# Attention in a hybrid diffusion step: steps of two query tiles in a written-out rotation, the scores of two heads on the two halves of the array, and the left half of the output weights 512 columns wide

## The chip, the cores and the metric

The kernel runs on one core of one Trainium2 chip. The metric is device microseconds of one execution, median over the runs shown. The engines are TensorE (PE, with its weight loads as a row of their own, PEld), VectorE (DVE), ScalarE (ACT), GpSimd (POOL) and SyncE (SP), which issues most DMAs.

## The reference

Two layers of a backbone act on 128 context tokens and 1024 sample tokens of width 1024, in float32. Layer 0 projects the modulated input once (`h @ w_in`, 3584 columns) and feeds a convolution branch and an attention branch, both gated; their outputs side by side (512 + 512 columns) go through one 1024 x 1024 output projection. Layer 1 is a pooling mixer with its own 1024 x 1024 output projection. What the change touches is the attention of layer 0 and the two output projections:

```
q = rms_norm(q, q_norm); k = rms_norm(k, k_norm)          # 8 heads of 64
# context tokens (128): plain attention
p = softmax(q @ k.T * 64**-0.5);  y = p @ v
# sample tokens (1024, a 16 x 64 grid): each block of 16 columns of a row sees
# an 8-row x 32-column window of keys (256) and all 128 context keys, in one softmax
s_win = where(col_ok, q @ k_win.T * 64**-0.5 + bias, -inf)
s_ctx = q @ k_ctx.T * 64**-0.5
p = softmax(concat(s_win, s_ctx));  y = p_win @ v_win + p_ctx @ v_ctx
# each layer's end
z = concat(y_conv * silu(ga), y_att * silu(gb));  out = z @ w_out
y = x + gate * out
```

## The kernel before

Every large product in float32 is made of three products of rounded parts (`float32r`): a number is split into a high part `hi` and the rest `lo`, and `hi*hi + hi*lo + lo*hi` is summed in one PSUM bank. `split` (L183) makes the parts of a weight unit of 1024 columns per partition: a copy on ACT, a subtraction on DVE.

The program is a list of items (L1164 to L1205), each with the weights that it needs; `ensure` loads and splits weights one or two items ahead. Items before the attention project the input (L225, 384 moving columns a matmul, and L232, 256 columns). A scheduler of the language (`schedule_with_timeline_sim=True`) moves the instructions on every engine, so an engine's order isn't the order of the code. PSUM has eight banks: four under the name `mm`, two `tp`, two `cv`.

Attention works on pairs of heads, `pr` = 0 to 3, and for each pair on two halves of the grid, `hf` = 0 and 1, with four query tiles of 128 (`j` = 0 to 3) each: 32 calls of `attn_tile` (L873). In one call:

- L883: for each head `e` of the pair two matmuls of 512 keys. The first has 128 rows: the stationary operand holds the head's `q` high part in 64 partitions and its low part in the other 64, the moving operand holds the same `k` high part twice. The second has 64 rows, `q` high times `k` low.
- L889 on DVE adds the bias and takes the extreme of each row; L893 on ACT takes the exponential and its sum; L894 on DVE takes the reciprocal; L895 on POOL multiplies.
- L898 transposes the probabilities in four 128 x 128 matmuls a head into a `tp` bank, which ACT copies out (L899).
- L905 multiplies with the values, the two heads on the two column halves of the array, 128 columns a matmul; L913 on DVE multiplies the result into the gated `za`.

`prep` (L791) turns the normalised `q` and `k` of a pair round (L806, L819), splits them on POOL and DVE, and copies `k` high to the other 64 partitions by a DMA (L843). The keys of the context cache stand ahead of the 1024 keys and behind them. `attn_prompt` (L916) does the context tokens. `bias_load` (L744) and `v_load` (L778) fetch the next pair's bias and value windows through SP; the value windows have one pair of buffers.

The output projection of layer 0 is `out0` (L1022), of layer 1 `out1` (L1048), nine tiles of 128 tokens each. For each tile `out_right` (L1006) makes columns 512 to 1023 in 24 matmuls of 512 columns, `out_left` (L995) columns 0 to 511 in two blocks of 24 matmuls of 256 columns.

## Time and profile before

| | us |
|---|---|
| median of 3 runs | 1037.79 (1035.22 to 1043.5) |
| profiled execution: time, its span | 1037.07, 1035.3 |
| PE busy | 999.0 (96%) |
| DVE, ACT, POOL busy | 615.3 (59%), 421.7 (41%), 406.1 (39%) |
| first score matmul of the attention (L883) | 439.74 |
| first matmul of the output projection of layer 0 (L1010) | 579.96 |
| last value matmul of the attention (L905) | 602.4 |

The span is cut by PE's work: input projections to 439 us, attention from 439 to about 602, the output projection of layer 0 mixed in from 580 and alone from 607 to about 718, the matmuls of layer 1 to 929, its output projection to the end. The profiled execution lies 0.7 us under the median. PE's matmuls are pipelined: the time that one takes from its neighbours is read from start to start, not from its own duration, which is longer.

### The profile page before, as it was taken

The page shows a single profiled execution, that of the slowest core. Times are in us where ns is not written, and L with a number is a line of the kernel's source. Part 1 is how long each engine was busy: PE and PEld are TensorE (multiplying, and loading weights), DVE is VectorE, ACT ScalarE, POOL GpSimd, SP SyncE. Part 2 cuts the span into 40 slices and gives each one's busy share as a digit, 9 for nine tenths or more (in the row PEclk, how much of TensorE's full clock was granted, in tenths as well). Part 3 has the DMA queues.
Part 4 walks back from the last instruction along what each step waited for, and adds up shares of the span by engine and source line. Part 5 has one row for each costly group of instructions (what it writes and reads, how often), then busy time and mean ns, then how long its engine had stood idle before and what let it go on. Part 6 is the DMA issues. An engine that isn't in the chain of part 4 may idle for free.

```text
span 1035.3 us, 17567 instructions
## 1 busy us (share of the span) xinstructions
PE 999.0 (96%) x6732; PEld 897.6 (87%) x6732; DVE 615.3 (59%) x1315; ACT 421.7 (41%) x851; POOL 406.1 (39%) x529
## 2 busy tenths in 40 slices
PE   5897999999999999999998999999999999999998
PEld 3786888899999999956665689999999999998997
DVE  3577999999833444475675455466354455586322
ACT  3374666765211443276675633244222222231010
POOL 2264879998533110564673324452000000003322
PEclk9998999999999999999998999999999999999999
DMA  9969554144211101325338132133111111133221
GB/s 299 330 174 331 177 214 143 52 154 142 62 51 44 41 21 52 86 65 144 88 107 202 66 115 84 68 113 103 41 51 41 51 42 51 51 113 107 98 82 62
DMA packets 90223, 111.74 MB, mean 108 GB/s; under 512 B 10828, under 2 KB 77260, under 8 KB 90027
## 3 DMA queue, kind: packets, MB, share of 16 engines
q1 hardware_dynamic: 84587, 95.93, 29.8%
q0 software_dynamic: 3216, 12.32, 3.6%
q10 hardware_dynamic: 2336, 2.36, 0.7%
q8 instruction: 53, 0.87, 0.4%
q14 instruction: 31, 0.25, 0.1%
HBM read 94.64 MB, written 21.57 MB: 112 GB/s over the span
## 4 chain that ended last, share of the span: by engine, by line
PE 86%; DMA 8%; SPq 2%; DVE 2%; POOL 1%; issue 1%; ACT 0%; ACTq 0%; POOLq 0%; DVEq 0%
PE mm L225 36%; PE mm L232 15%; PE mm L1010 9%; PE mm L1000 9%; PE mm L883 4%; PE cv L905 4%; PE tp L898 3%; DMA wada<-in_w_ada 2%; PE mm L1155 2%; DMA tbias<-in_rpb 2%; PE tp L335 2%; DMA raw<-in_w_out 1%; DMA k<-k 1%; DMA vwin<-in_cache_v 1%; SPq L294 1%; DMA wad<-in_w_ada 1%
## 5 line engine op out<-in xcount | busy, mean ns | idle before, releaser
L225 PE MATMUL mm<-h,whi 128*128 128x384 f32 x1536 | 396.9, 338 | 1.2 <-ACT whi L186 1.0
L225 PEld LDWEIGHTS mm<-h,whi 128*128 128x128 f32 x1536 | 276.6, 188 | 8.2 <-ACT gr L467 2.6
L225 PE MATMUL mm<-h,wlo 128*128 128x384 f32 x768 | 257.3, 336 | 0.3 <-DVE wlo L187 0.3
L469 POOL TENSOR_TENSOR zc<-zc,gr 128x384 f32<-128x384 f32 x138 | 150.2, 1090 | 31.9 <-ACT gr L467 22.9
L232 PE MATMUL mm<-whi,h 128*128 128x256 f32 x864 | 157.1, 284 | 0.0
L225 PEld LDWEIGHTS mm<-h,wlo 128*128 128x128 f32 x768 | 144.3, 188 | 1.3 <-issue 0.7
L232 PEld LDWEIGHTS mm<-whi,h 128*128 128x128 f32 x864 | 135.1, 192 | 3.9 <-issue 2.0
L232 PE MATMUL mm<-wlo,h 128*128 128x256 f32 x432 | 122.2, 283 | 0.0
L1000 PE MATMUL mm<-whi,zs 128*128 128x256 f32 x576 | 108.6, 284 | 0.0
L187 DVE TENSOR_TENSOR wlo<-raw,whi 128x1024 fp32r<-128x1024 f32 (+1 forms) x56 | 69.1, 1236 | 52.7 <-ACT whi L186 52.5
L480 DVE SCALAR_TENSOR_TENSOR cv<-u,convw,cv 128x384 f32<-128x384 f32 (+2 forms) x208 | 95.1, 512 | 0.9
L1010 PE MATMUL mm<-wrh,zs 128*128 128x512 f32 x288 | 93.4, 394 | 0.5 <-POOL wrh L981 0.5
L1000 PEld LDWEIGHTS mm<-whi,zs 128*128 128x128 f32 x576 | 91.7, 191 | 1.3 <-issue 0.2
L1017 POOL TENSOR_TENSOR y<-y,og 128x512 f32<-128x512 f32 x34 | 49.5, 1459 | 101.1 <-DVE og L1015 95.3
L186 ACT CAST whi<-raw 128x1024 fp32r<-128x1024 f32 (+1 forms) x56 | 56.9, 1016 | 64.0 <-PE mm L225 23.6
L232 PEld LDWEIGHTS mm<-wlo,h 128*128 128x128 f32 x432 | 82.9, 192 | 0.0
L1000 PE MATMUL mm<-wlo,zs 128*128 128x256 f32 x288 | 81.4, 283 | 0.0
L467 ACT ACTIVATE gr<-u,convw 128x384 f32<-128x384 f32 (+2 forms) x128 | 64.3, 531 | 30.7 <-POOL zc L469 30.2
L895 POOL TENSOR_SCALAR p<-p,st 128x512 f32<-128x512 f32 x64 | 49.7, 783 | 48.9 <-DVE st L894 40.9
L1015 DVE TENSOR_TENSOR og<-mm,gr 128x512 f32<-128x512 f32 x34 | 23.2, 688 | 70.0 <-PE mm L1010 39.0
L1010 PEld LDWEIGHTS mm<-wrh,zs 128*128 128x128 f32 x288 | 53.8, 188 | 10.8 <-POOL wrh L981 0.7
L449 ACT ACTIVATE th<-mm 128x384 f32<-128x384 f32 x48 | 23.5, 489 | 84.6 <-PE mm L225 80.2
(197 smaller groups left out, 1539.5 us busy)
## 6 DMA issues: line engine op xcount, KB each, us to landing
raw<-in_w_in SPq DMA_DIRECT2D x28, 512.0 KB
wad<-in_w_ada SPq DMA_DIRECT2D x16, 768.0 KB
wada<-in_w_ada SPq DMA_DIRECT2D x16, 512.0 KB
raw<-in_w_in SPq DMA_DIRECT2D x32, 256.0 KB
raw<-in_w_out SPq DMA_DIRECT2D x16, 512.0 KB
vw<-vwin SPq DMA_DIRECT2D x8, 640.0 KB
y0scr<-y POOLq DMA_DIRECT2D x9, 512.0 KB, 3.0
y<-y0scr SPq DMA_DIRECT2D x9, 512.0 KB
```

The lines of the kernel that those rows point to most:

```text
L186: se.copy(hi[:, :n], raw[:, :n])
L187: ve.tensor_tensor(lo[:, :n], raw[:, :n], f(hi[:, :n]), ALU.subtract)
L225: te.matmul(out, wsl(units, a, k, c0, P), hsl(hs, b, k, g), start=(k == 0 and i == 0), stop=(k == nk - 1 and i == 2))
L232: te.matmul(out, hsl(hs, p, k, g, a, P), wsl(units, q, k, 0, 256), start=(k == 0 and i == 0), stop=(k == 7 and i == 2))
L467: se.activation(pr[:, o : o + n], src, AF.Copy, scale=w)
L469: gp.tensor_tensor(z, z, pr, ALU.add)
L480: ve.scalar_tensor_tensor(zp if k == 30 else acc, src, convw[:, c, k : k + 1], zp if k == NPTS[c] else acc, ALU.mult, ALU.add)
L883: te.matmul(bs[e].rearrange("p (r c) -> p r c", c=32), qs[e][h, qo], kv, start=(i == 0), stop=(i == 1))
L895: gp.tensor_scalar(p2[:, e, :], p2[:, e, :], st[:, 4 + e : 5 + e], 0.0, ALU.mult, ALU.add)
L1000: te.matmul(b[:, blk * 256 : (blk + 1) * 256], zs[p][:, k, :], wsl(WL[blk], q, k, 0, 256), start=(k == 0 and i == 0), stop=(k == 7 and i = ...
L1010: te.matmul(b, zs[p][:, k, :], WR[q][k // 3][:, k % 3, :], start=(k == 0 and i == 0), stop=(k == 7 and i == 2))
L1017: gp.tensor_tensor(yv, yv, t, ALU.add)
```

## The change

The attention is written as a rotation. Its unit is a step of two query tiles of one pair and half: 16 steps, `STEPS`. In turn `s` of the loop PE does the scores of step s+1, the values of step s-1 and the transposes of step s, and then a piece of work for the context tokens or for the next pair. On PE, ACT and DVE the instructions keep the order in which the code writes them (`manual_schedule`); POOL and SP are still ordered by the scheduler.

- Scores: `q` and `k` of both heads lie in one tile each, head 0 in partitions 0 to 63, head 1 in 64 to 127. A tile of queries takes three products a head of 64 rows each, 512 keys wide, and the two heads' matmuls stand next to each other and write different banks. The second copy of `k` high and its DMA are gone.
- `prep` is cut into five pieces, spread over the turns of the pair before. ACT writes the high part straight from PSUM, DVE the low part from PSUM; these wait in `cv` banks.
- Of a step's four blocks of transposed probabilities, three go to banks `tp`, `tp`, `cv` and are copied by ACT, the fourth goes to a `tp` bank again and is copied by DVE. Values of two tiles share one bank.
- The context tokens' attention is in four pieces, one a turn.
- Value windows have two pairs of buffers. The right half of the output weights of layer 0 is loaded ahead and split on POOL and DVE alone, a quarter in each turn of the last pair.
- `out_left` makes 512 columns in 24 matmuls; the weights of the left half come in units of two row blocks by 512 columns (last tile of layer 1: still 256).

```diff
-    def split(raw, n=WUNIT):
+    def split(raw, n=WUNIT, c=256):
...
-        return hi.rearrange("p (k c) -> p k c", c=256), lo.rearrange("p (k c) -> p k c", c=256)
+        return hi.rearrange("p (k c) -> p k c", c=c), lo.rearrange("p (k c) -> p k c", c=c)
...
+        if srcs and srcs[0].shape[1] == 512:
+            for k0 in range(0, srcs[0].shape[0] // P, 2):
+                raw = wp.tile([P, WUNIT], F32, tag="raw", bufs=2, name=nm("raw"))
+                sy.dma_start(raw.rearrange("p (k c) -> p k c", c=512), srcs[0][k0 * P : (k0 + 2) * P, :].rearrange("(k p) c -> p k c", p=P))
+                raws.append((raw, WUNIT, 512))
...
-    VS = (6, 7)
-    QS = ((2, 3), (10, 11), (2, 3), (10, 11))
-    KS = ((4, 5), (12, 14), (4, 5), (12, 14))
-    KL = 16
+    QS = ((2, 3), (10, 11))
+    KS = ((4, 5), (None, 12))
+    VS = ((6, 7), (14, 16))
...
+        def two_parts(b, hi, lo, sc_):
+            se.activation(hi, b, AF.Copy, scale=sc_)
+            return lambda: ve.scalar_tensor_tensor(lo, b, sc_, f(hi), ALU.mult, ALU.subtract)
+        def q_half(i):
+            if i == 0:
+                st["q"] = [slot(x, F32R, "q")[:, :D] for x in QS[pr % 2]]
+            b = bank("cv")
+            for t in range(4):
+                o = b.rearrange("p (j r c) -> p r j c", j=4, c=16)[:, 2 * t : 2 * t + 2, :, :]
+                te.transpose(out=o, in_=qk_at(4 * i + t, pr)[:, 0:P], identity=ident)
+            o = slice(i * 512, (i + 1) * 512)
+            return two_parts(b, st["q"][0][:, o], st["q"][1][:, o], qn8)
+        def k_half(i):
+            b = bank("cv")
+            for t in range(4):
+                te.transpose(out=b[:, t * P : (t + 1) * P], in_=qk_at(4 * i + t, pr)[:, P : 2 * P], identity=ident)
+            if i == 0:
+                st["k"] = [slot(x, F32R, "k") if x is not None else gr_tile(F32R)[:, :SLOT] for x in KS[pr % 2]]
             o = slice(256 + i * 512, 768 + i * 512)
+            return two_parts(b, st["k"][0][:, o], st["k"][1][:, o], kn)
+        def rest():
+            qc = tmp("qc")
+            ck = qc[:, 2 * P : 3 * P]
+            last["ck"] = sy.dma_start(ck, A["cache_k_0"][0].rearrange("m h d -> m (h d)")[:, pr * P : (pr + 1) * P]).ins
+            b = bank("cv")
+            te.transpose(out=b[:, 0:P], in_=qk_at(8, pr)[:, 0:P], identity=ident)
+            te.transpose(out=b[:, P : 2 * P], in_=qk_at(8, pr)[:, P : 2 * P], identity=ident)
+            te.transpose(out=b[:, 2 * P : 3 * P], in_=ck, identity=ident)
+            se.activation(qc[:, 0:P], b[:, 0:P], AF.Copy, scale=qn8)
+            se.activation(qc[:, P : 2 * P], b[:, P : 2 * P], AF.Copy, scale=kn)
+            cx = b[:, 2 * P : 3 * P].rearrange("p (r w) -> p r w", w=32).unsqueeze(2).broadcast_to([P, 4, 2, 32])
+            kh, kl = st["k"]
+            hv, lv = (x[:, 0:256].rearrange("p (r a w) -> p r a w", a=2, w=32) for x in (kh, kl))
+            se.copy(hv, cx)
+            qkT[pr] = (*st["q"], kh, kl, qc[:, : 2 * P])
+            def later():
+                ve.tensor_tensor(lv, cx, f(hv), ALU.subtract)
+                for x in (kh, kl):
+                    gp.tensor_scalar(x[:, 1280:1536], f(x[:, 0:256]), 1.0, 0.0, ALU.mult, ALU.add)
+            return later
+        return [lambda: q_half(0), lambda: q_half(1), lambda: k_half(0), lambda: k_half(1), rest]
...
+    def scores(step, mem=None):
...
+        def matmuls(i):
+            j = j0 + i
+            bs = [bank("mm"), bank("mm")]
+            qo = slice(hf * 512 + j * P, hf * 512 + (j + 1) * P)
+            for n, (q, k) in enumerate(((qh, kh), (qh, kl), (ql, kh))):
+                for e in range(2):
+                    kv = k[H[e], o : o + 1024].rearrange("p (r c) -> p r c", c=64)[:, :, CB[j] : CB[j] + 32]
+                    te.matmul(bs[e].rearrange("p (r c) -> p r c", c=32), q[H[e], qo], kv, start=(n == 0), stop=(n == 2))
+            if mem is not None:
+                ps.append(mem[:, i * 1024 : (i + 1) * 1024].rearrange("p (e k) -> p e k", e=2))
+            else:
+                ps.append(wp.tile([P, 2, 512], F32, tag="whi", bufs=4, name=nm("p")))
+            sts.append(small(8, "st"))
             for e in range(2):
+                ve.tensor_tensor_reduce(
+                    out=ps[i][:, e, :], in0=bs[e], in1=bias[hf, e][:, JT[j], :], scale=-1.0, scalar=3e38, op0=ALU.add, op1=ALU.min,
+                    accum_out=sts[i][:, e : e + 1],
+                )
+        def exp(i, e):
+            p, st = ps[i][:, e, :], sts[i]
+            se.activation(p, p, AF.Exp, bias=st[:, e : e + 1], scale=-1.0, accum_out=st[:, 2 + e : 3 + e])
+        def norm(i):
+            st = sts[i]
+            ve.reciprocal(st[:, 4:6], st[:, 2:4])
+            for e in range(2):
+                gp.tensor_scalar(ps[i][:, e, :], ps[i][:, e, :], st[:, 4 + e : 5 + e], 0.0, ALU.mult, ALU.add)
+        return matmuls, exp, norm, ps
...
+    def values(step, pts, vw):
+        pr, hf, j0 = step
         ob = bank("cv")
         order = (4, 0, 1, 2) if hf == 0 else (1, 2, 3, 4)
+        for i in range(2):
+            for n, x in enumerate(order):
+                for e in range(2):
+                    te.matmul(
+                        ob[64 * e : 64 * e + 64, i * P : (i + 1) * P], vw[j0 + i][x][:, 64 * e : 64 * e + 64],
+                        pts[i][:, e, n * P : (n + 1) * P], start=(n == 0), stop=(n == 3),
+                    )
+        def gate():
+            r = 0
+            for zp, m in za_tok(pr, hf * 512, 512):
+                nr = m // 64
+                zv = zp.rearrange("p (r c) -> p r c", c=64)[:, :, 16 * j0 : 16 * j0 + 32].rearrange("p r (j c) -> p r j c", j=2)
+                ov = ob[:, : 2 * P].rearrange("p (j r c) -> p r j c", j=2, c=16)[:, r : r + nr, :, :]
+                ve.tensor_tensor(zv, ov, zv, ALU.mult)
+                r += nr
+        return gate
...
+    def prompt_attention(pr):
+        qp = qkT[pr][4]
+        pp = tmp("pp")
+        st = small(8, "st")
+        def first():
+            bs = [bank("cv"), bank("tp")]
+            for e in range(2):
+                te.matmul(bs[e][:, :P], qp[64 * e : 64 * e + 64, :P], qp[64 * e : 64 * e + 64, P : 2 * P], start=True, stop=True)
+            for e in range(2):
+                ve.tensor_reduce(st[:, e : e + 1], bs[e][:, :P], AX.X, ALU.max)
+            ve.tensor_scalar(st[:, 2:4], st[:, 0:2], -1.0, None, ALU.mult)
+            for e in range(2):
+                se.activation(pp[:, e * P : (e + 1) * P], bs[e][:, :P], AF.Exp, bias=st[:, 2 + e : 3 + e], accum_out=st[:, 4 + e : 5 + e])
+        def second():
+            ve.reciprocal(st[:, 6:8], st[:, 4:6])
+            for e in range(2):
+                gp.tensor_scalar(pp[:, e * P : (e + 1) * P], pp[:, e * P : (e + 1) * P], st[:, 6 + e : 7 + e], 0.0, ALU.mult, ALU.add)
...
+        return first, second, third, fourth
+    STEPS = [(pr, hf, j0) for pr in range(4) for hf in range(2) for j0 in (0, 2)]
...
+        first = hold["S"] = scores(STEPS[0], gr_tile())
+        for i in range(2):
+            first[0](i)
+            for e in range(2):
+                first[1](i, e)
+            first[2](i)
+        E = mybir.EngineType
+        with tc.manual_schedule(engines={E.PE, E.Activation, E.DVE}):
...
+    def attention_steps():
+        n = len(STEPS)
+        sc_, vw, pts = {0: hold["S"]}, {0: hold["V"]}, {}
+        pieces, later, right = [], [], None
+        for s in range(n + 1):
+            i, pr = s % 4, s // 4
+            while later:
+                later.pop(0)()
+            nxt = None
+            if s + 1 < n:
+                nxt = sc_[s + 1] = scores(STEPS[s + 1])
+                nxt[0](0)
+                nxt[0](1)
+                nxt[1](0, 0)
+                nxt[1](0, 1)
+                nxt[1](1, 0)
+                if pr < 3 and i in (0, 2):
+                    bias_load(pr + 1, i // 2)
+            if i == 0 and pr < 4:
+                pieces = prep(pr + 1) if pr < 3 else []
+                prompt = prompt_attention(pr)
+            gate = values(STEPS[s - 1], pts.pop(s - 1), vw[STEPS[s - 1][0]]) if s else None
+            if nxt:
+                nxt[2](0)
+            if gate:
+                gate()
+            if s == n:
+                break
+            ps = sc_.pop(s)[3]
+            pt = pts[s] = [wp.tile([P, 2, 512], F32, tag="wlo", bufs=4, name=nm("pt")) for _ in range(2)]
+            tbs = [bank("tp"), bank("tp"), bank("cv")]
+            for x in range(3):
+                turn(tbs[x], ps[x // 2][:, x % 2, :])
+            for x in range(2):
+                se.copy(pt[0][:, x, :], tbs[x])
+            if nxt:
+                nxt[1](1, 1)
+            tb = bank("tp")
+            turn(tb, ps[1][:, 1, :])
+            se.copy(pt[1][:, 0, :], tbs[2])
+            ve.tensor_copy(pt[1][:, 1, :], tb)
+            if nxt:
+                nxt[2](1)
+            prompt[i]()
+            for piece in pieces[2 * i : 2 * i + 2]:
+                later.append(piece())
+            if i == 2 and pr < 3:
+                vw[pr + 1] = v_load(pr + 1)
+            if pr == 3:
+                if i == 0:
+                    right = load_right(0, (13, 15, 17, 2, 3, 4))
+                hold["R"] = next(right)
...
-                if k % 2:
+                if k % 2 and l:
                     se.copy(hi[k // 3][:, k % 3, :], rv[:, k - k0, :])
...
-    def out_left(zs, WL, blks=(0, 1)):
+    def out_left(zs, WL, c0=0, n=512):
         b = bank("mm")
-        for blk in blks:
-            for k in range(8):
-                for i, (p, q) in enumerate(((0, 0), (0, 1), (1, 0))):
-                    te.matmul(
-                        b[:, blk * 256 : (blk + 1) * 256], zs[p][:, k, :], wsl(WL[blk], q, k, 0, 256),
-                        start=(k == 0 and i == 0), stop=(k == 7 and i == 2),
-                    )
+        for k in range(8):
+            for i, (p, q) in enumerate(((0, 0), (0, 1), (1, 0))):
+                te.matmul(b[:, c0 : c0 + n], zs[p][:, k, :], WL[k // 2][q][:, k % 2, c0 : c0 + n], start=(k == 0 and i == 0), stop=(k == 7 and i == 2))
         return b
...
-    items.append(([A["w_out_0"][:, 0:256]], keep("L0")))
+    items.append(([A["w_out_0"][0:512, 0:512]], keep("L0")))
...
+    items.append(([A["w_out_0"][512:1024, 0:512]], keep("L1", go_out0)))
```

On PE the rows change so. A tile and a half in pair 1 before (L883 scores, L905 values, L898 transposes; `k_5261` and `k_5262` are the high parts of head 0 and head 1, doubled, `kl` the low parts):

```order
L905 MATMUL cv_5318<-pt_5296,vw_4841 64x128 x7
L898 MATMUL tp_5352<-ident,p_5335 128x128 x4
L883 MATMUL mm_5494<-k_5262,q_5220 128x512
L883 MATMUL mm_5494<-kl_5263,q_5220 128x512
L905 MATMUL cv_5358<-pt_5336,vw_4843 64x128
L898 MATMUL tp_5382<-ident,p_5375 128x128 x4
L905 MATMUL cv_5358<-pt_5336,vw_4843 64x128 x7
L898 MATMUL tp_5392<-ident,p_5375 128x128 x4
L883 MATMUL mm_5533<-k_5261,q_5219 128x512
L883 MATMUL mm_5533<-kl_5263,q_5219 128x512
```

Scores of 128 and of 64 rows take turns there, and values, transposes and scores of different tiles stand between each other in small groups.

The second tile of a step, and what stands behind it, after the change (L877 scores, L913 values, L904 transposes; `mm_5195` and `mm_5196` are the banks of the two heads, `k_4792` and `q_4771` high parts, `k_4793` and `q_4772` low parts):

```order
L877 MATMUL mm_5195<-k_4792,q_4771 128x512
L877 MATMUL mm_5196<-k_4792,q_4771 128x512
L877 MATMUL mm_5195<-k_4793,q_4771 128x512
L877 MATMUL mm_5196<-k_4793,q_4771 128x512
L877 MATMUL mm_5195<-k_4792,q_4772 128x512
L877 MATMUL mm_5196<-k_4792,q_4772 128x512
L913 MATMUL cv_5220<-pt_5134,vw_4817 64x128 x8
L913 MATMUL cv_5220<-pt_5135,vw_4817 64x128 x8
L904 MATMUL tp_5244<-ident,p_5093 128x128 x4
L904 MATMUL tp_5245<-ident,p_5093 128x128 x4
L904 MATMUL cv_5246<-ident,p_5105 128x128 x4
L904 MATMUL tp_5262<-ident,p_5105 128x128 x4
```

All scores have 64 rows now and stand in pairs of heads; the kinds of work stand in blocks, three a turn. (Step 0 alone is outside the fixed order, and the scheduler has put its second tile head after head.)

On ACT, one turn of pair 0 after the change, with the two high parts of the next pair's `k` at its end (L892 exponentials, L1033 and L1038 copies of transposed probabilities, L804 high parts):

```order
L892 ACTIVATE p_5093,st_5094<-p_5093,st_5094 128x512 x2
L892 ACTIVATE p_5105,st_5106<-p_5105,st_5106 128x512
L1033 COPY pt_5134<-tp_5136 128x512
L1033 COPY pt_5134<-tp_5137 128x512
L892 ACTIVATE p_5105,st_5106<-p_5105,st_5106 128x512
L1038 COPY pt_5135<-cv_5138 128x512
L804 ACTIVATE gr_5172<-cv_5167,V 128x512
L804 ACTIVATE gr_5172<-cv_5175,V 128x512
```

Three exponentials stand ahead of the first two copies, and a fourth ahead of the third copy; before the change exponentials and copies of single heads took turns as the scheduler placed them.

More of the change, by code (lines that the diff above doesn't have):

```diff
@@ new lines, in exp, with turn @@
+        def exp(i, e):
[7 more added lines that the diff above has]
+        return matmuls, exp, norm, ps
+    def turn(tb, p):
+        for x in range(4):
+            te.transpose(out=tb[:, x * P : (x + 1) * P], in_=p[:, x * P : (x + 1) * P], identity=ident)
@@ L941, in attention_ahead @@
         elif g == 1:
-            prep(0)
+            for piece in prep(0):
+                piece()()
             with tc.issue_after(last["ck"]):
```

180 lines of the change are left out of this document (36 added, 144 removed).

## The prediction, made before the changed kernel ran

> **What bounds the kernel now.** I read the page's sums and its chain of waits first, then a table of windows over the attention and what follows it, then groups and timelines inside. From the page:
>
> ```profile
> span 1035.3 us, 17567 instructions
> ...
> PE 86%; DMA 8%; SPq 2%; DVE 2%; POOL 1%; issue 1%; ACT 0%; ACTq 0%; POOLq 0%; DVEq 0%
> ```
>
> PE carries 86% of the chain. The table of windows asks whether that holds in the stretch that changes (columns: window, length, busy time of PE, PEld, DVE, ACT and POOL with their instructions, granted clock, DMA share):
>
> ```profile
> 439.30:480.00 40.70, 39.26 (x251) 24.77 (x250) 27.20 (x94) 26.91 (x69) 24.54 (x37) 1.00 0.33 91
> ...
> 520.00:560.00 40.00, 34.42 (x216) 22.28 (x214) 26.73 (x79) 24.83 (x60) 26.94 (x36) 0.91 0.59 137
> ...
> 580.00:607.00 27.00, 27.00 (x209) 21.34 (x208) 11.20 (x28) 12.92 (x23) 4.50 (x6) 1.00 0.32 103
> 607.00:718.00 111.00, 110.26 (x727) 102.39 (x726) 62.70 (x88) 40.45 (x88) 50.24 (x62) 1.00 0.27 97
> ```
>
> PE is full, the others stand at about two thirds. From 520 to 560 PE loses 5.6 us and the granted clock falls to 0.91. The groups between 439.3 and 607 say why, and what of this stretch is not attention:
>
> ```profile
> L883 PE MATMUL mm<-k,q 128*128 128x512 f32 x64 | 31.9, 498 | 5.4 <-DMA k<-k 4.0 <-DVE st L894 1.1 <-issue 0.2
> ...
> L1010 PE MATMUL mm<-wrh,zs 128*128 128x512 f32 x25 | 8.6, 409 | 0.0
> ...
> L1010 PE MATMUL mm<-wrl,zs 128*128 128x512 f32 x13 | 5.1, 392 | 0.0
> ...
> L1000 PE MATMUL mm<-whi,zs 128*128 128x256 f32 x26 | 5.2, 286 | 0.0
> ...
> L1000 PE MATMUL mm<-wlo,zs 128*128 128x256 f32 x13 | 3.6, 290 | 0.0
> ```
>
> One wait of 4.0 us is for the DMA that copies `k`; the change removes it. For the pitch of the two kinds of output matmul, a piece of PE's timeline (start, length, count; five matmuls of 512 columns lie from the first row to the second):
>
> ```profile
> 645.60 0.39 PE L1010 MATMUL mm<-wrl,zs 128*128 128x512 f32 x1
> ...
> 646.73 0.28 PE L1000 MATMUL mm<-whi,zs 128*128 128x256 f32 x1
> 646.85 0.28 PE L1000 MATMUL mm<-wlo,zs 128*128 128x256 f32 x1
> ```
>
> 512 columns take 1.13 / 5 = 0.226 us, 256 take 0.12. So of the 167.7 us between 439.3 and 607 the output projection has 38 x 0.226 + 39 x 0.12 = 13.3 us, and the attention 154.4 us, waits included. That is the stock from which the change can take.
>
> **The attention on PE.** Its pitches, from one stretch of PE's and PEld's timelines:
>
> ```profile
> 457.87 0.50 PE L883 MATMUL mm<-k,q 128*128 128x512 f32 x1
> 458.30 0.50 PE L883 MATMUL mm<-gr,q 64*128 64x512 f32 x1
> 458.73 1.09 PE L905 MATMUL cv<-pt,vw 128*64 128x128 f32 x14
> 459.75 0.66 PE L898 MATMUL tp<-ident,p 128*128 128x128 f32 x4
> 460.16 0.48 PE L883 MATMUL mm<-k,q 128*128 128x512 f32 x1
> ...
> 457.87 0.19 PEld L883 LDWEIGHTS mm<-k,q 128*128 128x128 f32 x1 [0.25 <-ACT qc L844]
> 458.30 0.18 PEld L883 LDWEIGHTS mm<-gr,q 64*128 64x128 f32 x1 [0.25 <-issue]
> ```
>
> A score matmul of 512 columns takes 0.43 us, nearly twice the 0.226 of the output matmul as wide. PEld shows the reason: each load of weights starts together with its own matmul, after 0.25 us of idleness, so the load lies in the path; 128-row and 64-row matmuls take turns. Twelve 64-row matmuls in a row don't change the shape. Two heads in different halves do run together in this trace (context scores, 64 rows, two passes a head):
>
> ```profile
> 439.32 0.49 PE L921 MATMUL mm<-qc 64*128 64x128 f32 x4
> 439.74 0.50 PE L883 MATMUL mm<-k,q 128*128 128x512 f32 x1
> ...
> 465.09 0.48 PE L921 MATMUL mm<-qc 64*128 64x128 f32 x2
> 465.50 0.43 PE L905 MATMUL cv<-pt,vw 128*64 128x128 f32 x2
> ```
>
> Four passes of both heads took 0.42 us, two passes of one head 0.41: the second head was free. So I price a pair of score matmuls at 0.226 us. The bounds are 0.226 (paired, loads hidden) and 0.86 (two single ones at 0.43); I take the lower, because the two causes of 0.43 that the rows show are gone.
>
> [...]
>
> PE's sum for a step: six pairs 1.36 + 0.2 for the change of shape (0.43 - 0.226) = 1.6; values of two tiles: seven pairs of passes took 1.02 us, changes of shape included, sixteen take 2.0 to 2.3, say 2.1; transposes 4 x 0.41 = 1.65. Together 5.35, x 16 = 85.6. `prep` of three pairs is 19 transposes each at 0.1: 6. Context tokens, four times 0.42 for the scores, 0.2 for two transposes, about 0.4 for the values (as L905's passes) and a change of shape: 5. PE's own floor is 97 us, and 7 more for filling (first scores, four bias additions, exponentials, the scaling, with PE partly idle) and draining: **104**.
>
> **The ring through the other engines.** With PE 40% shorter, the others come near. Their rows (groups over the same stretch, then ACT's and DVE's timelines for the pitch, then a group of the whole span, L1015, and one more of the stretch, L982):
>
> ```profile
> L895 POOL TENSOR_SCALAR p<-p,st 128x512 f32<-128x512 f32 x64 | 49.7, 783 | 48.9 <-DVE st L894 40.9 <-PE cv L905 3.3 <-DVE st L858 2.6
> ...
> L894 DVE RECIPROCAL st<-st 128x1 f32<-128x1 f32 x64 | 9.2, 156 | 4.2 <-ACT p L893 3.9
> ...
> L842 DVE TENSOR_TENSOR kl<-cr,k 64x256 fp32r<-64x256 f32 x8 | 4.6, 592 | 0.1
> ...
> L857 ACT ACTIVATE p<-mm,st 128x128 f32<-128x128 f32 x8 | 2.9, 368 | 1.0 <-DVE st L856 1.0
> ...
> L854 DVE TENSOR_REDUCE st<-mm 128x1 f32<-128x128 f32 x8 | 2.1, 282 | 2.9 <-PE mm L921 2.9
> ...
> 454.98 1.28 ACT L828 ACTIVATE kr<-mm,V 128x512 f32<-128x512 f32 x2
> 456.12 1.11 ACT L899 COPY pt<-tp 128x512 f32<-128x512 f32 x2
> 457.06 0.33 ACT L834 COPY cr<-mm 128x128 f32<-128x128 f32 x1
> ...
> 460.46 0.71 ACT L893 ACTIVATE p<-p,st 128x512 f32<-128x512 f32 x1
> 461.17 0.56 ACT L899 COPY pt<-tp 128x512 f32<-128x512 f32 x1
> ...
> 468.74 0.69 DVE L889 CUSTOM_DVE_ANT_0 p<-mm,bias 128x512 f32<-128x512 f32 x1
> 469.35 0.29 DVE L854 TENSOR_REDUCE st<-mm 128x1 f32<-128x128 f32 x1
> ...
> L1015 DVE TENSOR_TENSOR og<-mm,gr 128x512 f32<-128x512 f32 x34 | 23.2, 688 | 70.0 <-PE mm L1010 39.0 <-PE mm L1000 29.8 <-POOL rstd L114 0.9
> L982 DVE TENSOR_TENSOR wrl<-raw,wrh 128x512 fp32r<-128x512 f32 x8 | 6.1, 806 | 2.6 <-POOL wrh L981 2.6
> ```
>
> Pitches: bias addition 0.61, exponential with its sum 0.71, copy 0.47, high part 0.57. A DVE copy or low part from PSUM isn't in the trace; L1015, which reads PSUM at the same size, gives 0.69 (it has a second operand, so rather less; with 0.61, the pitch of L889, a step loses 0.1 to 0.2).
>
> The fixed order makes a ring. The fourth block of transposes needs the `tp` bank that ACT's first copy frees, and that copy stands behind three exponentials, which follow the bias additions. The next step's additions stand on DVE behind the copy of the fourth block. From a step's first addition: 0.65 + 3 x 0.71 = 2.8, copy 0.5, transposes 0.41, DVE copy 0.69, reciprocal 0.16, three to four handovers at an estimated 0.1: 5.0. On ACT alone: 2.8 + 0.47 x 2 + 0.71 + 0.47 = 4.9. So a turn without extras takes PE's 5.35. Extras, per pair:
>
> - Turn 0: maxima of the context tokens on DVE, 2 x 0.28 and a small one as the reciprocal, then two exponentials of 0.37 that overlap at their ends, 0.6, then the two high parts of `q` on ACT 2 x 0.57 and the last low part 0.69, ahead of the next additions: 5.0 + 0.7 + 0.6 + 1.15 + 0.7 = 8.1. PE stands meanwhile before the values of the next turn, whose `cv` bank a low part still reads.
> - Turn 1: 4.9 + 1.15 + 0.7 = 6.75.
> - Turn 2: 4.9 + small copies 1.0 + the context's low part 0.59 = 6.5.
> - Turn 3: 5.35.
>
> That is 26.7 a pair, 80 for three. The last pair has three rings without `prep` but with two low parts of the output weights a turn (2 x 0.81): 3 x 7 + 0.6 = 21.6. With filling 7 and draining 3: **112** us. Whole durations in place of pitches (0.72 + 0.09 + 0.1 on some eight links) give 119, PE alone 104. I take 112. Hidden I count three things. POOL's scaling (2 x 0.78 after each reciprocal) has the next scores and values, 1.6 + 2.1 us, ahead of its reader. The bias loads on SP start after the last addition that reads the old bias, nearly three turns or some 19 us before their use. The value windows have their own buffers, and the right half's weights are asked for before the attention. If the first cover fails, each turn pays its overhang (rival 4).
>
> **The left half.** 48 matmuls at 0.12 = 5.76 become 24 at 0.226 = 5.42: 0.34 us a tile, 9 tiles in layer 0 and 8 in layer 1: 5.7 us, as both stretches are full on PE (110.26 of 111 us above). I take 5, some changes between the two halves being less smooth; nothing is the other bound, if the loads of the split left half come late.
>
> **The sum.** 154.4 - 112 = 42.4 from the attention, 5 from the left half: 1037.1 - 47.4 = 989.7 for the profiled execution. The median of the runs is 0.7 higher: **990 us**.
>
> **Rivals and chances.** (1) The ring as above, 985 to 998: 0.47. (2) PE's floor holds, handovers hide: attention 100 to 104, 975 to 985: 0.2. For it speaks that durations overlap on ACT and DVE. (3) Pairs cost about 0.43, because loads show or because heads run one after the other at 0.226 each: 6 x 0.2 x 16 = 19 us more on PE, 104 + 19 = 123, above the ring: 1001, with spread to 1008: 0.15. [...] (4) The fixed order meets a wait that I don't see (a `cv` bank held by a late low part, POOL, bias) of 1 to 2 us in each turn: attention 128 to 144, 1006 to 1022: 0.1. (5) Slower: the 64-row matmul keeps 0.43 us whatever stands beside it, and heads run singly. For it: every 64-row score in the trace takes that. Against it: PEld's rows, and the context scores. Then a step's scores take 12 x 0.43 + 0.2 = 5.4, PE's step 9.1, the attention 16 x 9.1 + 11 + 7 = 164; 1037.1 + 9.6 - 5 = 1042. It decides from a step of 8.8 us on. 0.05. The rest, 0.03, is a change that breaks something outside: the output weights late, the clock down.
>
> The three runs before spread over 0.8%, so 1% is about what can be told from no change. Faster by more than 1% (below 1027): 0.92; within: 0.05; slower: 0.03. A range that leaves out the slow rival and the ends of (2) and (4): 972 to 1016.
>
> **What would show it.** Right: score pairs a few ns apart and 0.23 us from pair to pair, PE idle in turns 0 to 2 of each pair before scores, waiting for DVE; last values near 551 us. Wrong: pairs at 0.43 or more (rivals 3, 5); PE without gaps (2); waits on POOL or a DMA in each turn (4); a granted clock under 0.95 in the attention; pitch of the left half other than 0.226.

## The result, and the profile after

The changed kernel took **996.79 us** (median of four executions, 995.80 to 998.65), the kernel before beside it 1040.64: a ratio of 0.9582 (95% interval 0.9525 to 0.9638), 4.2% faster. Forecast were 990, in a range of 972 to 1016. The profiled execution took 996.42 us, its span 994.6 against 1035.3. From the page of the changed kernel, the span and the chain of waits by engine:

```profile
span 994.6 us, 16662 instructions
...
PE 83%; DMA 5%; DVE 4%; ACT 3%; SPq 3%; issue 2%; POOL 1%; DVEq 0%; POOLq 0%; ACTq 0%
```

PE still carries the chain, but DVE and ACT, 2% and 0% before, now hold 7% of it. The table of windows has the attention from its first score to its last value, and what follows up to layer 1's middle (window, length, busy time of PE, PEld, DVE, ACT and POOL with their instructions, granted clock, DMA share):

```profile
439.96:558.32 118.36, 104.66 (x1060) 81.56 (x1059) 80.71 (x253) 87.33 (x222) 57.82 (x88) 1.00 0.41 123
558.32:717.10 158.78, 156.09 (x791) 138.25 (x792) 89.23 (x134) 55.13 (x114) 51.52 (x69) 1.00 0.26 88
```

Without the two output matmuls that lie in it (0.7 us start to start), the attention takes 117.7 us. Before it was 154.4: 36.7 less. Added from start to start without the waits, the scores fell from 55.6 to 27.7 us and the values from 44.4 to 30.4, though the same value matmuls run; they now stand in blocks, and no run tests that cause alone. The transposes of the probabilities kept theirs (32.1 and 32.8), and PE's idle time between the first score and the last value rose from 7.0 to 13.7 us. The clock stays at 1.00 all through, where it was 0.91 in one stretch. The left matmuls, added from start to start, fell from 52.7 to 49.3 us in layer 0 and from 51.9 to 49.4 in layer 1: 5.9 less. Against that stands a new wait of 1.95 us ahead of the first left matmul (for ACT's high part of these weights, which itself waits for its DMA); waits in layer 1's output are 1.1 us shorter, the attention begins 0.7 us later. -36.7 - 5.9 + 1.95 - 1.1 + 0.7 = -41.05, of the 40.7 that the span lost.

PE's groups in the attention show what is left of its idleness:

```profile
L913 PE MATMUL cv<-pt,vw 128*64 128x128 f32 x512 | 31.5, 276 | 0.0
L904 PE MATMUL tp<-ident,p 128*128 128x128 f32 x180 | 25.8, 279 | 2.7 <-POOL p L898 2.3 <-ACT pt L1033 0.3
L877 PE MATMUL mm<-k,q 64*128 64x512 f32 x128 | 21.4, 418 | 2.1 <-ACT k L840 1.4 <-DVE st L885 0.6
L877 PE MATMUL mm<-gr,q 64*128 64x512 f32 x64 | 12.3, 422 | 2.8 <-ACT gr L840 2.8
...
L813 PE MATMUL cv<-ident,qk 128*128 128x128 f32 x24 | 3.9, 287 | 3.3 <-ACT pp L943 1.7 <-ACT pt L1038 1.6
L820 PE MATMUL cv<-ident,qk 128*128 128x128 f32 x24 | 3.8, 280 | 1.5 <-ACT pt L1038 1.5
```

The score matmuls themselves wait for ACT's copy of `k` (L840, a piece of `prep`), and the transposes of the next pair's `q` and `k` (L813, L820) wait for `cv` banks that ACT has not read yet: those of the third block (L1038) and of the context tokens' scores (L943). Together these are 9.0 us of the 13.7. The pitch of the pairs, from PE's timeline of one step (start, length, count):

```profile
480.86 0.50 PE L877 MATMUL mm<-gr,q 64*128 64x512 f32 x2
481.20 0.40 PE L877 MATMUL mm<-k,q 64*128 64x512 f32 x2
481.43 0.64 PE L877 MATMUL mm<-gr,q 64*128 64x512 f32 x4
481.91 0.40 PE L877 MATMUL mm<-k,q 64*128 64x512 f32 x2
482.14 0.40 PE L877 MATMUL mm<-gr,q 64*128 64x512 f32 x2
482.47 0.98 PE L913 MATMUL cv<-pt,vw 128*64 128x128 f32 x14
```

Rows of two are the two heads; from one pair to the next it is 0.23 to 0.24 us, 0.34 behind the change of shape: twelve matmuls in 1.6 us.

**A turn, read through.** A turn is counted here from a step's first bias addition to the next step's. Turn 0 of the third pair, from DVE's timeline:

```profile
503.21 0.69 DVE L885 CUSTOM_DVE_ANT_0 p<-mm,bias 128x512 f32<-128x512 f32 x1 [0.43 <-PE mm L877]
...
507.75 0.69 DVE L1039 COPY pt<-tp 128x512 f32<-128x512 f32 x1 [1.54 <-PE tp L904]
...
508.93 0.40 DVE L941 TENSOR_SCALAR st<-st 128x2 f32<-128x2 f32 x1
510.78 1.41 DVE L805 SCALAR_TENSOR_TENSOR q<-cv,vq,q 128x512 fp32r<-128x512 f32 x2 [1.46 <-ACT q L804]
512.11 0.68 DVE L885 CUSTOM_DVE_ANT_0 p<-mm,bias 128x512 f32<-128x512 f32 x1
```

The same stretch on ACT and on PE:

```profile
508.03 0.59 ACT L1038 COPY pt<-cv 128x512 f32<-128x512 f32 x1
509.36 0.37 ACT L943 ACTIVATE pp<-cv,st 128x128 f32<-128x128 f32 x1 [0.74 <-DVE st L941]
...
510.06 1.26 ACT L804 ACTIVATE q<-cv,vq 128x512 fp32r<-128x512 f32 x2
...
503.71 1.97 PE L913 MATMUL cv<-pt,vw 128*64 128x128 f32 x32
505.61 1.09 PE L904 MATMUL tp<-ident,p 128*128 128x128 f32 x8
506.54 0.60 PE L904 MATMUL cv<-ident,p 128*128 128x128 f32 x4
507.09 0.63 PE L904 MATMUL tp<-ident,p 128*128 128x128 f32 x4
...
508.67 0.66 PE L813 MATMUL cv<-ident,qk 128*128 128x128 f32 x4 [0.54 <-ACT pt L1038]
509.87 0.66 PE L813 MATMUL cv<-ident,qk 128*128 128x128 f32 x4 [0.55 <-ACT pp L943]
510.46 1.69 PE L877 MATMUL mm<-k,q 64*128 64x512 f32 x12
```

8.90 us: the ring to DVE's copy ends after 5.15, then maxima and their negation, the exponentials of the context tokens, the high parts, the low parts, the next addition. Up to the context tokens' scores PE shows no idle time, and DVE's copy waits 1.54 us for PE's last transposes: this first part goes at PE's own pace. Only the 3.75 us behind it are a chain through DVE and ACT, and there PE waits twice for a bank. Turn 2 ends at the scores of the next pair's first step, which need the copy of `k`; PE's timeline there, ahead of the third pair:

```profile
495.94 1.91 PE L877 MATMUL mm<-k,q 64*128 64x512 f32 x12 [1.42 <-ACT k L840]
```

Added up from the first additions, the four turns of a pair take 8.89, 7.23, 7.53 and 5.94 us, 29.6 in all, the same in each pair to 0.2 us.

### The profile page after: what moved, and what is told of

Read it like the earlier page. It is cut to its first block, busy times and chain, and to the rows that moved or that the text cites. A ratio compares the mean times of both kernels' runs of the same rounds, so it can differ in the third digit from the quotient of the medians.

```text
span 994.6 us, 16662 instructions
## 1 busy us (share of the span) xinstructions
PE 951.6 (96%) x6388; PEld 865.3 (87%) x6388; DVE 599.2 (60%) x1231; ACT 408.3 (41%) x827; POOL 366.9 (37%) x485
## 4 chain that ended last, share of the span: by engine, by line
PE 83%; DMA 5%; DVE 4%; ACT 3%; SPq 3%; issue 2%; POOL 1%; DVEq 0%; POOLq 0%; ACTq 0%
PE mm L232 39%; PE mm L239 16%; PE mm L1101 10%; PE mm L1094 9%; PE mm L1246 2%; PE tp L342 2%; ACT p L892 2%; SPq L757 2%; DMA raw<-in_w_out 1%; DVE p L885 1%; DMA bias<-texp 1%; PE mm L877 1%; DMA wad<-in_w_ada 1%; DMA raw<-in_w_in 1%; PE tp L904 1%
## 5 line engine op out<-in xcount | busy, mean ns | idle before, releaser
L1094 PE MATMUL mm<-whi,zs 128*128 128x512 f32 (+1 forms) x304 | 92.8, 379 | 2.0 <-ACT whi L186 2.0
L1094 PEld LDWEIGHTS mm<-whi,zs 128*128 128x128 f32 x304 | 56.0, 188 | 12.7 <-ACT whi L186 2.2
L898 POOL TENSOR_SCALAR p<-p,st 128x512 f32<-128x512 f32 x60 | 44.3, 752 | 53.0 <-DVE st L896 45.3
L1094 PE MATMUL mm<-wlo,zs 128*128 128x512 f32 (+1 forms) x152 | 57.3, 378 | 0.0
```

Of the source, the lines that this page charges most:

```text
L898: gp.tensor_scalar(ps[i][:, e, :], ps[i][:, e, :], st[:, 4 + e : 5 + e], 0.0, ALU.mult, ALU.add)
L1094: te.matmul(b[:, c0 : c0 + n], zs[p][:, k, :], WL[k // 2][q][:, k % 2, c0 : c0 + n], start=(k == 0 and i == 0), stop=(k == 7 and i == 2))
```

## The experiments

My theory: the attention is paced by a ring through PE, ACT and DVE, whose extras (`prep` and the context tokens) lie in series in turns 0 to 2. The main rival: PE's own work sets the time (its floor of about 104 us), and the waits are small change. Times are medians; each run had the kernel before beside it, with 1036 to 1040 us. The ratios are known to about 0.5% either way, so two of these runs that lie 3 or 4 us apart can't be told from each other by their times; what they show is read from the turns and waits in their profiles.

**The left half in 256 columns again** (`out_left`; loads and split as changed):

```
...
+        for c in range(c0, c0 + n, 256):
...
-                te.matmul(b[:, c0 : c0 + n], zs[p][:, k, :], WL[k // 2][q][:, k % 2, c0 : c0 + n], ...
...
+                    te.matmul(b[:, c : c + 256], zs[p][:, k, :], WL[k // 2][q][:, k % 2, c : c + 256], ...
```

> The changed kernel (996.8 us), with its left half of the output weights multiplied in two passes of 256 columns again; loads and split stay in 512 columns. If the width pays by PE's pitch (48 x 0.12 us against 24 x 0.226 us a tile, 17 tiles, and the profiles of the two kernels show 3.4 and 2.5 us less in these matmuls): 5 to 6 us slower, 1002 to 1003. If the loads and splits of the left half set that stretch (PE waits 1.95 us for them before the first left matmul of layer 0): 0 to 3 us slower.

Measured: 1006.50 us, ratio 0.9713 (0.9672 to 0.9753). 9.7 us slower than the changed kernel by the medians, more than either theory had. The attention is unchanged (118.3 us), the stretch behind it 5.9 us longer and layer 1's 5.5. The left matmuls took 105.9 us from start to start against 98.7, so 7 of the 11.4 us are theirs. What is new beside them is the clock, in the table of windows at the start of this output:

```profile
560.00:562.00 2.00, 0.85 (x4) 0.74 (x5) 0.87 (x1) 1.16 (x2) 0.00 (x0) 0.95 0.58 216
562.00:564.00 2.00, 2.00 (x7) 1.54 (x5) 2.00 (x6) 0.93 (x1) 0.00 (x0) 0.50 0.21 33
564.00:566.00 2.00, 2.00 (x8) 1.63 (x7) 1.09 (x1) 0.00 (x0) 0.00 (x0) 0.70 0.64 238
```

After an idle stretch of 2.63 us the clock was granted at half for 3.41 us, and again at 903 us after 1.35 us. Some of the 7 us lies in these stretches as well: the kernel before, at full clock, had 104.6 us of left matmuls. Against the changed kernel's 98.7 that is 5.9 us, so the width is worth the 5 to 6 us of the first theory; the surplus goes with waits and the clock.

**The two heads one after the other** in the queue (`scores`):

```
-    for n, (q, k) in enumerate(((qh, kh), (qh, kl), (ql, kh))):
-        for e in range(2):
+    for e in range(2):
+        for n, (q, k) in enumerate(((qh, kh), (qh, kl), (ql, kh))):
```

> The changed kernel, with the twelve score matmuls of a step in the order head after head in place of pairs. If pairs run at once and a lone 64-row matmul also takes 0.226 us (loads hidden): PE gets 6 x 0.226 = 1.36 us more in each of 16 steps, 22 us if PE carries each step, 8 to 16 us if waits that are there now (15 us of idle PE in the attention) take up a part: 1005 to 1019. [...] If pairs don't run at once: no difference.

Measured: 1000.35 us, ratio 0.9656 (0.9615 to 0.9697); none of the prices came. PE's timeline of the step quoted above, in this kernel:

```profile
481.88 0.51 PE L877 MATMUL mm<-gr,q 64*128 64x512 f32 x2
482.23 0.40 PE L877 MATMUL mm<-k,q 64*128 64x512 f32 x2
482.46 0.64 PE L877 MATMUL mm<-gr,q 64*128 64x512 f32 x4
```

The queue holds three matmuls of the first head and then three of the second, and still they ran in pairs, 4 to 15 ns apart, with 0.23 us from one row of two to the next (482.23 to 482.46): the second head's first matmul, three places behind the first head's in the queue, started with it. The edit undid nothing, so it does not price the pairs. Of its 96 possible pairs 84 ran together (92 in the changed kernel, counted by starts under 30 ns apart). The 3.6 us more go with two drops of the clock in the attention, at 446 and 528 us, which the changed kernel's profile does not have.

**The fourth block of transposes in a bank of the scores:**

```
-            tb = bank("tp")
+            tb = bank("mm")
             turn(tb, ps[1][:, 1, :])
```

> The changed kernel, with the fourth block of transposes of a step in a bank of the scores (free by then) in place of the bank that ACT's first copy has to free. If the ring through ACT's copy holds PE in each turn, as the prediction had it: the fourth block starts 0.2 to 0.4 us earlier in each of 15 turns, 3 to 6 us faster, 991 to 994. If PE's own work is the ring in turn 3 and the waits behind the extras of turns 0 to 2 take up the rest: 0 to 2 us faster.

Measured: 998.55 us, ratio 0.9637 (0.9600 to 0.9674): no gain. Turns 0 and 3 got 0.1 us shorter each, so the bank that ACT's first copy frees is not what holds PE: twelve transposes before it take as long. This link of the predicted ring is worth 0.1 us a turn, not 0.2 to 0.4. But PE now stood idle 1.67 us ahead of the scores at the end of turn 2, where it was 1.42, and this followed:

```profile
496.00:498.00 2.00, 1.02 (x6) 0.67 (x8) 0.42 (x1) 0.93 (x4) 1.88 (x4) 1.00 0.44 137
498.00:500.00 2.00, 2.00 (x14) 1.22 (x12) 1.69 (x5) 0.96 (x3) 0.00 (x0) 0.54 0.29 81
500.00:502.00 2.00, 2.00 (x27) 2.00 (x26) 0.92 (x5) 1.27 (x4) 0.91 (x2) 0.61 0.32 100
502.00:504.00 2.00, 2.00 (x24) 1.83 (x20) 0.49 (x2) 0.96 (x3) 0.45 (x1) 1.00 0.12 36
```

The clock fell to half for 3.41 us in two of three pairs, and turn 3 took 7.4 us there in place of 5.9.

**The extras in another order:** preparation ahead of the context tokens in turns 0 and 2, the context tokens' scores in `mm` banks, the copy of `k` first:

```
...
+            if i % 2:
+                prompt[i]()
             for piece in pieces[2 * i : 2 * i + 2]:
                 later.append(piece())
-            prompt[i]()
+            if i % 2 == 0:
+                prompt[i]()
```

> The changed kernel, with the extras in another order: in turn 0 the transposes and high parts of q ahead of the context tokens' scores, maxima and exponentials (these in banks of the scores), in turn 2 the preparation ahead of the context tokens' transposes, and the copy of the context's k ahead of those of the context's q and k. If the chain through maxima, exponentials, high parts and low parts sets turn 0, and ACT's small copies turn 2 (PE waits 1.42 us for the copy of k): 1.6 us in turn 0 and 0.8 us in turn 2, three pairs: 7 us faster, 989 to 991. If PE's own order sets the time and these chains only fill gaps that come back: within 2 us of 996.8.

Measured: 997.95 us, ratio 0.9636 (0.9590 to 0.9683): no gain. The four turns of a pair take 8.49, 7.62, 7.27, 5.95 us: turn 0 gained 0.4 and turn 1 lost 0.4, turn 2 gained 0.25. The exponentials, now behind the high parts, hold two `mm` banks, so the scores of turn 0 took 2.84 us in place of 1.69 and the values came late. In turn 0 the low parts still stood behind the maxima on DVE. The links that I moved were not the only ones of their length.

**Preparation in the banks of the scores,** its transposes ahead of the fourth block (a piece now gives back its part on ACT, and that its low part):

```
...
+            acts = [piece() for piece in pieces[2 * i : 2 * i + 2]]
             tb = bank("tp")
             turn(tb, ps[1][:, 1, :])
...
+            for act in acts:
+                later.append(act())
             prompt[i]()
...
```

> The changed kernel, with the preparation of the next pair in banks of the scores, its transposes on PE ahead of the fourth block of transposes, its high parts on ACT ahead of the context tokens' exponentials (in turn 2 the copy of k first, those of the context's q and k a turn later). If the extras are dear because PE waits for banks that ACT's copies hold and because of their place in the order: turn 0 (from bias addition to bias addition) from 8.9 to 7.5 us, turn 1 from 7.2 to 6.5, turn 2 from 7.5 to 6.7, three pairs: 7 to 9 us faster than the changed kernel, 988 to 990. If gains in one turn are given back in the next, as in the run with the extras in another order: within 2 us of 996.8.

Measured: 1000.90 us, ratio 0.9642 (0.9597 to 0.9687). Turns 8.07, 9.57, 7.67, 6.12: turn 0 gained 0.8 as the theory had it in part, turn 1 lost 2.3, and the time shows no gain. PE's timeline shows where:

```profile
515.38 0.47 PE L881 MATMUL mm<-k,q 64*128 64x512 f32 x1 [1.27 <-DVE q L805]
516.04 1.54 PE L881 MATMUL mm<-k,q 64*128 64x512 f32 x5 [0.19 <-DVE q L805]
517.51 2.94 PE L917 MATMUL cv<-pt,vw 128*64 128x128 f32 x32
```

The second half of the scores now waits for `mm` banks that the low parts of `q` still read, and the values, 1.97 us elsewhere, take 2.94: the clock was at half from 516.12 on, and likewise at 454.68 and 485.40.

**All twelve score matmuls in one half of the array** (`k[H[e]`, `q[H[e]` became `k[H[0]`, `q[H[0]`):

> The changed kernel, with both heads' scores from the first head's rows, so that all twelve score matmuls of a step lie in one half of the array and run singly (what is computed for the second head of each pair isn't the attention). The first scores of the changed kernel show lone matmuls at 0.235 us. If that holds and PE sets the pace in turn 3 and the last pair, and waits for ACT cover a part elsewhere: 1.36 us a step where PE is full, 0.6 to 1.0 elsewhere, 12 to 20 us: 1009 to 1017. If pairing is worth nothing because the ring through ACT and DVE sets the pace everywhere: within 4 us of 996.8. [...]

Measured: 1017.89 us, ratio 0.9810 (0.9764 to 0.9857). PE's timeline of a step:

```profile
486.62 0.63 PE L877 MATMUL mm<-k,q 64*128 64x512 f32 x2
487.09 1.11 PE L877 MATMUL mm<-gr,q 64*128 64x512 f32 x4
488.04 0.63 PE L877 MATMUL mm<-k,q 64*128 64x512 f32 x2
```

One matmul now takes 0.237 us start to start ((488.04 - 486.62) / 6), with a load of its own into the same half (by the table of windows 188 loads for 190 matmuls of all kinds from 440 to 470 us), and nothing beside it. At 0.237 us, against 0.43 where the loads showed, the load was hidden here behind a matmul of the same half. The 0.43 of the kernel before then points to matmuls of 128 and of 64 rows taking turns, since each kind alone takes 0.226 to 0.237; no run changed the alternation alone. The attention got 27.3 us longer. Of these the clock at half for 23.9 us (at 470, 504, 525 and 545 us) explains up to 12, which leaves about 15, one a step: the pairs are worth that much directly, and more through the clock. The time lies just above the first theory's range, and the second is out.

**Without the preparation of the third and fourth pair:**

```
-                pieces = prep(pr + 1) if pr < 3 else []
+                pieces = prep(pr + 1) if pr < 1 else []
+                if 1 <= pr < 3:
+                    qkT[pr + 1] = qkT[1]
```

> The changed kernel without the preparation of q and k for the third and fourth pair, which use those of the second (their part of the attention isn't computed from their own q and k). If the extras stand in the chain with all their links: each of the two pairs that lose it falls from 29.6 to 24.5 us (turns of 6.1), 10 us faster, 986 to 988. If only PE's own work for it counts (19 transposes of 0.11 us a pair): 4 us faster, 992 to 994.

Measured: 984.83 us, ratio 0.9489 (0.9447 to 0.9530): 12.0 us faster than the changed kernel, above both theories and nearer the first. The first additions of three steps in a row:

```profile
472.00 0.69 DVE L885 CUSTOM_DVE_ANT_0 p<-mm,bias 128x512 f32<-128x512 f32 x1 [0.45 <-PE mm L877]
...
478.06 0.69 DVE L885 CUSTOM_DVE_ANT_0 p<-mm,bias 128x512 f32<-128x512 f32 x1
...
483.36 0.69 DVE L885 CUSTOM_DVE_ANT_0 p<-mm,bias 128x512 f32<-128x512 f32 x1 [0.19 <-PE mm L877]
```

Turns 6.06, 5.30, 5.80, 5.93: 23.1 a pair in place of 29.6, so `prep` costs 6.5 us a pair. 19 transposes at 0.11 would be 2.1 of it, the whole cost if only PE's own work counted. The tables of windows divide it, for four turns of the changed kernel and four without preparation (length, then busy PE):

```profile
473.62:503.21 29.59, 26.38 (x273) 20.66 (x271) 19.21 (x62) 22.02 (x56) 12.37 (x21) 1.00 0.41 114
...
472.00:495.10 23.10, 23.10 (x254) 18.59 (x252) 16.03 (x57) 18.80 (x49) 11.57 (x19) 1.00 0.47 129
```

3.3 us are busy PE (changes of shape and waits too short to show among them), 3.2 us are waits. So the extras do cost by their links, which the floor alone leaves out. But without them PE has no idle time left: a turn with next to nothing added, turn 1 at 5.30 us, goes at PE's pace, and the ring through ACT and DVE isn't longer than that.

**Without the fixed order** (`manual_schedule` taken off):

> The changed kernel without the fixed order: the same steps, and the scheduler orders PE, ACT and DVE. If the order written by hand is what makes the steps overlap: 1005 to 1030. If the gain comes from pairs of heads alone (scores and values together 42 us less on PE in the profiles): 990 to 1000.

Measured: 1005.90 us, ratio 0.9711 (0.9653 to 0.9768), 9 us slower than the changed kernel. PE waits less (8.5 us against 13.7 in the attention's stretch), but the score matmuls take 36.8 us from start to start in place of 27.7, since only 50 of 96 pairs still run together. In PE's order as built, 21 of the 32 tiles have three matmuls of one head ahead of three of the other, all but two with nothing between. The order alone isn't the loss, since the run with the heads one after the other kept 84 pairs with it. But in 18 of these 21 tiles the second head starts 0.13 us or more behind the first, and its matmuls fall between the first head's or behind them. In 16 of the 18 the second head has a wait for DVE of its own, and DVE's additions lie 0.61 us apart; in the fixed order most tiles have no such wait. That these waits are the cause is read from the order, not tested alone. A stretch of 6.83 us at half the clock, after two waits of 2.33 and 2.45 us, is in this run as well. The time lies at the near end of the first theory's range; what the order buys is pairs, not fewer waits.

**The changed kernel again, and the extras moved out of each other's way:** in turn 0 the first half of `q` ahead of the context tokens' scores, these in the two `tp` banks; in turn 1 the second half of `k` in a `tp` bank and ACT's high parts ahead of its copy of the third block; in turn 2 the copy of `k` first:

```
-            bs = [bank("cv"), bank("tp")]
+            bs = [bank("tp"), bank("tp")]
...
+            acts = [piece() for piece in pieces[2 * i : 2 * i + (1, 2, 1, 0)[i]]]
+            lows = [act() for act in acts] if i else []
             se.copy(pt[1][:, 0, :], tbs[2])
             ve.tensor_copy(pt[1][:, 1, :], tb)
+            if i == 0:
+                ctx = prompt[0]()
+                next(ctx)
+                acts += [piece() for piece in pieces[1:2]]
```

> The changed kernel itself once more, beside the next run on the same chip: 995 to 1000, ratio to the kernel before 0.958 to 0.966.

> The changed kernel, with the extras placed so that no transposes wait for a bank that a copy on ACT still holds, and no score for a bank of the extras: in turn 0 the first half of q ahead of the context tokens' scores, these in the two banks of the transposes; in turn 1 the second half of k in a bank of the transposes and ACT's high parts ahead of its copy of the third block; in turn 2 the context's k ahead of that copy and of the rest. If the 6.5 us a pair that the run without preparation saved are made of these waits and of this order: turn 0 from 8.9 to 7.7 us, turn 1 from 7.2 to 6.4, turn 2 from 7.5 to 6.3, 3.2 us a pair, three pairs: 9 to 10 us faster than the changed kernel beside it. If each gain comes back in the next turn, as in the two runs that moved the extras before, or the granted clock drops for it: within 4 us of it.

Measured, on one chip: the changed kernel 997.28 us (991.50 to 1000.72; ratio 0.9597, 0.9530 to 0.9665), this one 988.55 (three executions, 986.62 to 990.62; ratio 0.9516, 0.9461 to 0.9572; a fourth took 1881 us and is left out). 8.7 us faster, the fastest that computes everything. From PE's timeline, turn 0 of the third pair:

```profile
501.51 0.60 PE L813 MATMUL cv<-ident,qk 128*128 128x128 f32 x4
502.04 0.90 PE L942 MATMUL tp<-qc 64*128 64x128 f32 x4
502.87 0.66 PE L813 MATMUL cv<-ident,qk 128*128 128x128 f32 x4
503.45 1.69 PE L881 MATMUL mm<-k,q 64*128 64x512 f32 x12
```

No wait stands in brackets in these rows any more. Turns 7.78, 6.72, 6.31 and 5.94: 26.75 a pair, of which PE is busy 26.24:

```profile
470.43:497.17 26.74, 26.24 (x273) 20.99 (x271) 18.99 (x62) 22.07 (x56) 12.34 (x21) 1.00 0.49 136
```

PE's idle time in the attention fell from 13.7 to 5.8 us, the attention from 118.3 to 110.5, and PE's busy time stayed at 104.6 to 104.7: what the new places took away are waits. Part of this is lost behind the attention. The wait ahead of the first left matmul is 2.46 us here and 0.93 in the changed kernel beside it, and half the clock for 3.41 us follows, so the spans of these two profiles (994.0 and 988.8) differ by only 5.2 us.

## Why the prediction was right, and where it was off

- **The likeliest case was the one that came:** rival 1, a ring through ACT and DVE in fixed order, 985 to 998. The gain was 43.9 us by the medians, forecast 47.8; by the spans of the profiles it was 40.7, forecast 47.4. 996.8 lies near the upper end of this case, and inside it only because the filling of the rotation took 2.9 us less than put (below): that much is luck.
- **Stock and what is hidden.** The 154.4 us and the wait of 4.0 us for the DMA were rightly read. POOL, the bias loads and the value windows stayed hidden: POOL holds PE 2.3 us in all. The chain of waits does lead through the bias loads (by the page of the changed kernel 2% for SP's issues at L757 and 1% for the DMAs), but that is a meeting in time: without preparation, SP's row of these loads reads

```profile
473.95 5.50 SPq L757 DMA_DIRECT2D bias<-texp  x8
```

  and the addition at 478.06, quoted above, starts before the last of them is issued.
- **Pairs at 0.226:** right, 0.23 to 0.24. Rival 3 falls by the pairs and by the lone matmuls at 0.237; rival 5 falls by the same rows. Values were put at 2.1 us a step and took 1.9. Four transposes of 0.41 were put at 1.65; from start to start they took 2.05, short waits included.
- **The turn without extras:** 5.35 put, as PE's own sum, and 5.30 measured without `prep`, with PE full. The ring of 5.0 that was drawn for it never sets the pace, and its link through the fourth block's bank is worth 0.1 us. The handovers in it, put at 0.1 us each, were an estimate from no row; in turn 0 above ACT's exponential started 0.03 us after the negation's end on DVE (509.33 to 509.36). DVE's copy, priced at 0.69 with rather less expected for its one operand, took 0.69, and the next instruction started 0.61 after it (507.75 to 508.36), as behind a bias addition (503.21 to 503.83). Right in the forecast, then, is the chain of the extras, not a ring that turns slower than PE.
- **The step that was off is "Extras, per pair",** 26.7 us put and 29.6 measured. In turn 0 (8.1 against 8.9) the ring took 5.15 for 5.0, the negation of the maxima 0.40 where I took a reciprocal's 0.15, the two exponentials 0.7 for 0.6, the high parts 1.25 for 1.15. In turn 2 (6.5 against 7.5) I counted ACT's small copies, but not that the scores stand behind the last of them and take 1.3 us to the first addition; PE's wait of 1.42 is that. Turn 1 (6.75 against 7.2) has a wait for the bank of the third block, and turn 3 (5.35 against 5.9) the context tokens' values on PE. Times three this is 9 us; filling took 4.1 us in place of 7, the last pair with its drain 25.3 in place of 24.6. 117.7 - 112 = 5.7 us is the whole miss in the attention. Divided by PE, the 29.6 are 26.4 busy and 3.2 of waits; the prediction's terms make 24.7 of PE's work (four steps of 5.35, 2 for `prep`, 1.25 for the context tokens) and leave 2.0 for waits. So a good half of the miss is PE's own work, where the transposes took 0.4 us a step more than put and `prep` 3.3 us a pair for 2 (short waits included in both), and the rest is waits. Put out of each other's way, the extras gave 26.75, the 26.7 of the sum, but with PE busy for 26.24 of it: that the two agree is in part chance.
- **The left half:** 5.7 worked out, 5.9 in PE's time; the 1.95 us ahead of its first matmul is the lateness of the loads that I had named as the other bound.
- **Rival 2, PE's floor** of 104 us, is right as a floor: PE is busy for 104.7. It is the pace in turn 3 and in most of the last pair; 13.7 us of waits lie on top, 10.6 of them in turns 0 to 2 of the first three pairs. **Rival 4** came in a mild form: waits of 0.5 to 1.4 us, but for banks and copies of `prep`, not one in each turn.
- **Marks.** PE idle in turns 0 to 2: yes, but directly before scores in turn 2 alone, in turns 0 and 1 before the transposes of `q` and `k`, and for ACT's copies rather than for DVE. Last values at 558.3, not 551. Clock over 0.95: 1.00. Left pitch 0.226: 0.228.

## What to carry to other kernels

When a rotation in fixed order is no longer bound by one engine, cost each turn as a chain through all of them, and put into it what the in-order engine does between two links, its waits for banks included; whole durations give a good sum only if nothing shares a bank with a copy that stands later in another engine's order. Leave out one kind of extra work to price it before moving it about: here that gave 6.5 us a pair, half of it waits, while two reorderings by eye gave nothing and a third, made along the rows of the waits, gave 8.7 us. A small additional idle time on PE can cost more than itself through the clock (with the fourth block in a bank of the scores PE's wait grew from 1.42 to 1.67 us, the clock fell to half, and turn 3 took 7.4 us in place of 5.9), so a change that gathers PE's waits into one place should be read with the granted clock beside it.

## What the runs showed of the hardware

- **The clock fell to half behind idle stretches of PE of 1.35 to 2.63 us, but not behind each.** It went to half for 3.41 or 6.83 us after PE had stood idle for 1.35 us (left half, at 903 us), 1.42 (heads one after the other, at 528; scores in one half, at 470, 504 and 545), 1.45 in two pieces (preparation in the banks of the scores, three times), 1.67 (fourth block, twice), 2.45 (without the fixed order), 2.46 (extras out of each other's way) or 2.63 us (left half). It stayed full after 1.42 us three times and 1.95 once in the changed kernel, after the third stretch of 1.67, after 2.57 (extras in another order) and even after 3.09 (without preparation, ahead of the left half). And two drops, at 446 us with the heads one after the other and at 525 with the scores in one half, have no stretch over 0.55 us in the 3.4 us ahead of them. With preparation in the banks of the scores the three drops begin 30.72 us apart (454.68, 485.40, 516.12), nine times the 3.41 us that each lasted. What sets off a drop no run tried alone. With all scores in one half of the array the clock fell most often (23.9 us in the attention) though PE stood idle less there (10.0 us against 13.7); why was not tried either.
- **The spread between executions goes with it at most in part:** the changed kernel's second series ran 991.5, 995.7, 998.8 and 1000.7 us at mean clocks of 0.997, 0.993, 0.990 and 0.991, but the run with the extras out of each other's way 986.6, 988.6 and 990.6 at 0.993, 0.991 and 0.994.
- **Matmuls of the two halves did not start in the order of the queue:** with the heads one after the other, three of one head ahead of three of the other ran as three pairs, up to 15 ns apart, in 84 of 96 possible pairs (92 in the changed kernel). Three places ahead is as far as these runs went. In 18 of 21 tiles without the fixed order, where most second heads have a wait of their own, the same queue order gave no such pairs: the second head started 0.13 us or more behind the first.
